# Grouped-query attention of a hybrid trunk: scores by queries for the maxima, scores by keys for the values

## The chip, the cores and the metric

The kernel runs on one core of one Trainium2 chip. The metric is device microseconds of one execution of the whole program, the median over several runs. The core has five engines that work beside each other, each through its own instructions in order: TensorE (PE, matrix products into PSUM), VectorE (DVE), ScalarE (ACT), GpSimd (POOL, which here also issues the row gathers), and SyncE (SP, which issues most of the DMAs). Everything is float32.

## The reference, cut to what matters

A trunk of two layers works on two groups of tokens: a prompt of 128 tokens and a sample of 512 tokens, both of width 1024. In each layer four mixers (grouped-query attention, RWKV-7, neighbourhood attention, gated DeltaNet) of 256 columns each stand beside each other, their outputs go through `w_out`, and then a sparse expert layer (PEER) follows. The mixer of this case is the first one, for the sample: 4 query heads of 64 columns share 2 key/value heads, and each of the 512 queries attends in one softmax to the 512 latent keys and to 128 cached context keys.

```python
def blocked_attention(q, k, v):
    def one_block(qblk):
        s = jnp.einsum("bkgqd,bkld->bkgql", qblk, k).astype(jnp.float32) * scale
        p = jax.nn.softmax(s, axis=-1).astype(v.dtype)
        return jnp.einsum("bkgql,bkld->bkgqd", p, v)
    ...
def gqa_mixer(p, lp, ctx_kv):
    ...
    q = rms_norm(q, lp["gqa_q_norm"]); k = rms_norm(k, lp["gqa_k_norm"])   # then rotary
    o = blocked_attention(qh, jnp.concatenate([kh, k_ctx], axis=2),
                              jnp.concatenate([vh, v_ctx], axis=2))
```

## The kernel before

The program is written with tiles: pools hand out buffers, and a scheduler orders the instructions of each engine by priorities and by a simulated run. Every engine then works through its list in order. A tile that takes over a buffer waits until the last reader of the earlier tile is done.

The stages of the sample are, for each layer: `s_mix` (input projections, then the four mixers), then `s_peer` (`w_out`, norm, expert layer). In `s_mix` the RWKV steps (names `s_R`, `s_U`, `s_dS`, `s_S`, `s_O`), the DeltaNet inverse (`s_Yt` and `s_BK` on DVE and POOL, then `s_Z`, `s_TZ`, `s_W`, `s_u` on PE), the DeltaNet steps and the neighbourhood attention `na` (`s_ns`) are independent chains that the scheduler interleaves with the attention `gqa`. The prompt's expert layer runs beside them: `p_back` gathers 128 rows of `u` and 128 rows of `v` per layer, one row per token and step (`p_gr`, issued by POOL, into a ring of three buffers), and DVE adds each (`ph<-p_gr,pac,ph`, 128x1024). After its last row, `p_back` takes two more buffers of that ring for `p_x` and `p_g`, loaded by SP, adds the residual on DVE, and in layer 0 stores it (`pxs<-p_x`).

Before the change, `gqa` (L575 to L682) does the following for the sample. After norm and rotary, queries and keys are transposed to `qT` and `kT` (64 rows of one head group in each half of the partitions). Then a loop of 16 turns, over 4 query tiles `t` and 4 heads `h`, goes in two halves; `skewed` emits the scores of a turn ahead of the values of the turn before.

- `scores`: one product of 64 rows with 512 columns (latent keys) and one with 128 columns (context keys) into a pair of PSUM banks `s_sc`; DVE takes the row maximum over 640 columns (`s_gmx`, L656); ACT takes the exponential of 128x640 with the row sum (`s_pr`).
- `values`: `soft_T` transposes the five 128x128 blocks of `s_pr` on PE back into the banks of `s_sc` (L328), ACT copies them (`s_pT`, 128x512, and `s_pTb`, 128x128), and five products with 64 columns of values sum into `s_po`.
- After the fourth head of a tile: reciprocal of the sums (128x4), one multiplication (`s_oat`), two transposes, two copies into `mixA`.

`mix_out` stores each mixer's output to memory (`smix`). In `s_peer`, `w_out` (L1469 to L1495) loads it back (`s_mix<-smix`) and loads the weights (`s_wo<-in_w_out_dram`), both by SP; its first product `s_wo<-s_wo,s_mix` begins the rest of the layer.

## Time and profile before

| what | value |
|---|---|
| median of the runs | 4911.13 us (4857.45 to 4959.15, 3 runs) |
| span of the profiled execution | 4964.6 us |
| PE busy | 4286.4 us (86%) |
| DVE busy | 3412.8 us (69%) |
| ACT busy | 1456.1 us (29%) |
| POOL busy | 1877.7 us (38%) |
| mean granted clock of TensorE | 0.844 |

The profiled execution is about 1.1% above the median and about 0.1% above the slowest of the three runs. In the rows further down, PE's matrix products appear as records: a product of float32 operands has two records, a transpose one. `s_sc<-s_kT,s_qT` names the tile that is written and the tiles that are read. [...] The attention of layer 0 lies at about 797 to 982 us, that of layer 1 at about 3197 to 3375 us.

### The profile page before, as it was taken

How to read it: one execution, taken by the hardware profiler on the slowest of the kernel's cores; microseconds unless marked ns; L12 is line 12 of the kernel's file. 1: busy time of each engine (PE TensorE's matmuls, PEld its weight loads, DVE VectorE, ACT ScalarE, POOL GpSimd, SP SyncE). 2: the span in 40 equal slices, each digit the busy share in tenths (PEclk: the TensorE clock that was granted, in tenths of full speed). 3: DMA queues.
4: the chain of work that ended last, by engine and by line, in shares of the span. 5: the costliest groups of instructions: out<-in, count | busy, mean ns of one | idle time of the engine just before them, and what ended most of it. 6: DMA issues, size and time to landing. Idle time of an engine off the chain costs nothing. (4 is left out here: it accounts for less than half of the span.)

```text
span 4964.6 us, 64764 instructions
## 1 busy us (share of the span) xinstructions
PE 4286.4 (86%) x21406; PEld 2957.0 (60%) x21406; DVE 3412.8 (69%) x8434; ACT 1456.1 (29%) x4149; POOL 1877.7 (38%) x1696
## 2 busy tenths in 40 slices
PE   7888878877698989999993688898769999999989
PEld 4454556665466854666672355666547788577563
DVE  2337875655899875664568677655489998894884
ACT  3322333331111840211110331433211174351340
POOL 0004443232443335443435443423144344463543
PEclk8888975556899989999996778555689999999979
DMA  7767885577797989997998879636679889999877
GB/s 263 261 203 244 272 259 162 156 204 271 265 342 263 359 292 366 362 363 269 364 357 277 274 262 284 194 114 192 239 256 325 299 306 327 340 357 342 328 261 284
DMA packets 500348, 1384.67 MB, mean 279 GB/s; under 512 B 109552, under 2 KB 167856, under 8 KB 498992
## 3 DMA queue, kind: packets, MB, share of 16 engines
q0 software_dynamic: 221184, 805.40, 47.5%
q1 hardware_dynamic: 215472, 531.29, 30.3%
q10 hardware_dynamic: 63360, 43.85, 2.8%
q8 instruction: 172, 2.82, 0.2%
q14 instruction: 160, 1.31, 0.1%
HBM read 1323.41 MB, written 56.93 MB: 278 GB/s over the span
## 5 line engine op out<-in xcount | busy, mean ns | idle before, releaser
L321 PE MATMUL s_us<-s_hT,s_uT 128*128 128x256 f32 x4096 | 964.2, 389 | 47.5 <-ACT s_pa L310 31.3
L1765 POOL DMA_INDIRECT s_gr<-in_peer_v_dram,s_ig x512 | 631.6, 1234 | 736.6 <-DVE s_acc L307 354.0
L1765 POOL DMA_INDIRECT s_gr<-in_peer_u_dram,s_ig x512 | 596.1, 1164 | 827.3 <-DVE s_gr L307 375.1
L321 PEld LDWEIGHTS s_us<-s_hT,s_uT 128*128 128x128 f32 x4096 | 775.5, 194 | 179.0 <-ACT s_pa L310 37.6
L307 DVE SCALAR_TENSOR_TENSOR s_acc<-s_gr,s_gact,s_acc 128x1024 f32<-128x1024 f32 x508 | 650.2, 1280 | 210.2 <-DMA s_gr<-in_peer_v_dram,s_ig 204.6
L307 DVE SCALAR_TENSOR_TENSOR s_gr<-s_gr,s_h 128x1024 f32<-128x1024 f32 x512 | 617.4, 1216 | 170.8 <-DMA s_gr<-in_peer_u_dram,s_ig 170.2
L321 PE MATMUL s_out<-s_v,s_pa 128*128 128x512 f32 x1408 | 625.7, 603 | 3.5 <-ACT s_gstg L310 2.2
L321 PE MATMUL s_cm<-s_hT,s_w 128*128 128x512 f32 (+3 forms) x1664 | 537.0, 478 | 24.8 <-ACT s_stg L310 17.4
L1765 POOL DMA_INDIRECT p_gr<-in_peer_v_dram,pig x256 | 262.2, 1024 | 615.2 <-DVE ph L307 340.7
L321 PEld LDWEIGHTS s_out<-s_v,s_pa 128*128 128x128 f32 x1408 | 268.5, 193 | 326.2 <-issue 322.0
L1765 POOL DMA_INDIRECT p_gr<-in_peer_u_dram,pig x256 | 290.4, 1134 | 443.4 <-DVE p_gr L307 247.0
L321 PEld LDWEIGHTS s_cm<-s_hT,s_w 128*128 128x128 f32 (+1 forms) x1664 | 281.7, 197 | 244.1 <-issue 148.8
L307 DVE SCALAR_TENSOR_TENSOR p_gr<-p_gr,ph 128x1024 f32<-128x1024 f32 x256 | 311.8, 1220 | 156.7 <-DMA p_gr<-in_peer_u_dram,pig 156.1
L307 DVE SCALAR_TENSOR_TENSOR ph<-p_gr,pac,ph 128x1024 f32<-128x1024 f32 x254 | 325.2, 1280 | 123.3 <-DMA p_gr<-in_peer_v_dram,pig 121.2
L310 ACT ACTIVATE s_hot<-consts,s_gT 128x128 f32<-128x128 f32 x768 | 271.8, 391 | 310.2 <-PE s_G L321 308.5
L321 PEld LDWEIGHTS s_G<-s_hot 128*128 128x128 f32 x2048 | 296.1, 210 | 93.8 <-ACT s_hot L310 28.2
L321 PE MATMUL s_G<-s_hot 128*128 128x42 f32 (+2 forms) x2048 | 305.8, 298 | 49.1 <-DVE s_hot L304 25.7
L304 DVE TENSOR_SCALAR s_hot<-consts,s_gT 128x42 f32<-128x42 f32 (+2 forms) x1024 | 281.5, 327 | 14.7 <-PE s_G L321 14.1
L321 PE MATMUL s_out<-s_v,s_p 128*128 128x512 f32 x640 | 287.3, 594 | 1.8 <-DMA s_v<-in_peer_v_dram 1.8
L310 ACT ACTIVATE s_hot<-s_hot,ones 128x128 f32<-128x128 f32 x768 | 267.4, 388 | 1.3
L321 PEld LDWEIGHTS s_out<-s_v,s_p 128*128 128x128 f32 x640 | 119.2, 190 | 127.1 <-issue 119.4
L328 PE MATMUL s_xT<-consts,s_xn 128*128 128x128 f32 x128 | 29.5, 378 | 184.1 <-ACT s_acc L293 84.6
(705 smaller groups left out, 6051.8 us busy)
## 6 DMA issues: line engine op xcount, KB each, us to landing
s_uT<-in_peer_uT_dram SPq DMA_DIRECT2D x256, 512.0 KB
s_v<-in_peer_v_dram SPq DMA_DIRECT2D x256, 512.0 KB
s_wm<-in_w_mod_dram SPq DMA_DIRECT2D x96, 512.0 KB
s_w<-in_peer_wq_dram SPq DMA_DIRECT2D x54, 512.0 KB
p_w<-in_w_in_dram SPq DMA_DIRECT2D x50, 512.0 KB
s_w<-in_w_in_dram SPq DMA_DIRECT2D x50, 512.0 KB
p_w<-in_peer_wq_dram SPq DMA_DIRECT2D x32, 512.0 KB
sproj<-s_stg ACTq DMA_DIRECT2D x50, 256.0 KB
```

Of the source, the lines that this page charges most:

```text
L304: self.nc.vector.tensor_scalar(out=out, in0=a, scalar1=s1, scalar2=s2, op0=op0, op1=op1)
L307: return self.nc.vector.scalar_tensor_tensor(out=out, in0=a, scalar=s, in1=b, op0=op0, op1=op1, **kw)
L310: self.nc.scalar.activation(out, in_, f, **kw)
L321: i = self.nc.tensor.matmul(out, lhsT, rhs, start=start, stop=stop)
L328: i = self.nc.tensor.transpose(out, in_, self.ident[b : b + n, b : b + n])
L1765: nc.gpsimd.indirect_dma_start(out=u, out_offset=None, in_=self.ap[f"{table}{l}"], in_offset=o)
```

## The change

The sample's attention moves into a new function, `gqa_ctx`. The prompt keeps the old path.

- Each key tile `ka` (and `kac` for the context keys) holds one key head in its 64 partitions, zeros in the other 64, and ones in one row of those. The query tile `Q` is kept four times (key head, query head), 128 rows each.
- `maxima(h)`: for each of the four query tiles the same score products as before (64 rows, 512 and 128 columns), the same DVE maximum (negated), then a product of the maxima's column with the identity, which gives a row of 128; ACT copies the row (1x128) into the row of `Q` that meets the row of ones.
- `values(h)`: for each of the five key blocks one product of 128 rows, keys as the stationary operand, with all 512 queries (`s_sT`). The row of ones brings the negated maximum in. ACT takes the exponential, 128x512, and one product of a 128x128 block of `vb` (64 columns of ones beside 64 columns of values) with 512 columns sums into `s_po`. Half of its rows are the sums, the other half the outputs. DVE takes a reciprocal of 64x512 and multiplies 64x512 into `mixA`, which needs no transpose.
- The 88 transposes per layer, the exponentials of 128x640 with their sums, the copies `s_pT` and `s_pTb`, and the 80 products with 64 columns are gone. New are, per layer, 16 products with one stationary column, 16 copies of 1x128, 40 products of 128x128 with 512 columns, 20 exponentials of 128x512, 4 reciprocals and 4 multiplications of 64x512, and 10 memsets on POOL. The values are loaded in pieces of 64 columns.

```diff
@@ -586,10 +586,20 @@
                 self.stt(tab[i][:, 1, :, 0:32], sin, -1.0, g2, ALU.mult, ALU.mult)
                 self.tt(tab[i][:, 1, :, 32:64], sin, g1, ALU.mult)
         qr = [a.rearrange("p (t k d) -> p t k d", k=2, d=64) for a in st.a1("qr")]
-        kr, vt = st.a1("kr")
-        self.pload(st, vt, 3)
+        if st.ctx:
+
+            kr = st.u1("kr")
+            vb = [st.wp.tile([P, 11, 64], F32, tag="w", name=st.nm("vb")) for _ in range(2)]
+            for kv, v in enumerate(vb):
+                cs = slice(64 * kv, 64 * kv + 64)
+                nc.gpsimd.memset(v[:, 0:11:2], 1.0)
+                nc.sync.dma_start(v[:, 1:9:2], st.proj[3].rearrange("p (t c) -> p t c", c=P)[:, :, cs])
+                nc.sync.dma_start(v[:, 9], self.ap["cgv"][l, :, cs])
+        else:
+            kr, vt = st.a1("kr")
+            self.pload(st, vt, 3)
+            vt = vt.rearrange("p (t c) -> p t c", c=P)
         kr = kr.rearrange("p (t h d) -> p t h d", h=2, d=64)
-        vt = vt.rearrange("p (t c) -> p t c", c=P)
         for ch in range(3):
             sq, qn = st.a1("qsq")
             self.pload(st, qn, ch)
@@ -618,6 +628,9 @@
         if not st.ctx:
             nc.scalar.dma_start(self.out["gk"][l].rearrange("k n d -> n k d"), kr[:, 0])
             nc.scalar.dma_start(self.out["gv"][l].rearrange("k n d -> n k d"), vt[:, 0].rearrange("p (k d) -> p k d", k=2))
+        if st.ctx:
+            self.gqa_ctx(st, l, qr, kr, vb)
+            return
         qT = st.a1("qT")
         kT, kc = st.a1("kT")
         for j in range(3):
@@ -630,55 +643,75 @@
             else:
                 self.act(qT[j], ps[:, :T], AF.Copy, scale=0.125)
         mixT = st.a1("mixA")
-        if not st.ctx:
-            heads = []
-            for h in range(4):
-                kv, j = h // 2, h % 2
-                rows = slice(64 * kv, 64 * kv + 64)
-                heads.append((qT[j][rows], kT[rows], vt[:, 0, 64 * kv : 64 * kv + 64]))
-            self.full_attn(st, heads, ([0, 1], [2, 3]), mixT)
-            self.mix_out(st, 0, mixT)
-            return
-        kc, vc = kc[:, :P], kc[:, P : 2 * P]
-        nc.sync.dma_start(kc, self.ap["cgk"][l])
-        nc.sync.dma_start(vc, self.ap["cgv"][l])
-        acc = {}
-
-        def scores(i):
-            t, h = i // 4, i % 4
+        heads = []
+        for h in range(4):
             kv, j = h // 2, h % 2
             rows = slice(64 * kv, 64 * kv + 64)
-            q = qT[j][rows, t * P : (t + 1) * P]
-            ps = st.pair("sc")
-            self.mm(ps[:, :T], q, kT[rows])
-            self.mm(ps[:, T : T + P], q, kc[rows])
-            m = st.asmall("gmx", 1)
-            nc.vector.tensor_reduce(out=m, in_=ps[:, : T + P], axis=AX.X, op=ALU.max, negate=True)
-            pr = st.asmall("pr", T + P)
-            if h == 0:
-                acc[t] = st.asmall("gsm", 4)
-            self.act(pr, ps[:, : T + P], AF.Exp, bias=m, accum_out=acc[t][:, h : h + 1])
-            return pr, ps
-
-        def values(i, prs):
-            pr, ps = prs
-            t, h = i // 4, i % 4
-            kv = h // 2
-            pT = self.soft_T(st, [pr[:, :T], pr[:, T:]], [ps[:, :T], ps[:, T:]])
-            if h == 0:
-                acc["po"] = st.out_psum("po")
-            po, sm = acc["po"], acc[t]
-            for kk in range(5):
-                v = vt[:, kk, 64 * kv : 64 * kv + 64] if kk < 4 else vc[:, 64 * kv : 64 * kv + 64]
-                self.mm(po[:, h * 64 : (h + 1) * 64], pT[kk], v, kk == 0, kk == 4)
-            if h == 3:
-                nc.vector.reciprocal(sm, sm)
-                o = st.u1("oat")[:, :256]
-                self.tt(o.rearrange("p (h d) -> p h d", h=4), po[:, :256].rearrange("p (h d) -> p h d", h=4),
-                        sm.unsqueeze(2).to_broadcast([P, 4, 64]), ALU.mult)
-                self.to_mix(st, mixT, o, t, po[:, 256:])
-
-        skewed(4 * NT, scores, values)
+            heads.append((qT[j][rows], kT[rows], vt[:, 0, 64 * kv : 64 * kv + 64]))
+        self.full_attn(st, heads, ([0, 1], [2, 3]), mixT)
+        self.mix_out(st, 0, mixT)
+
+    def gqa_ctx(self, st, l, qr, kr, vb):
+
+
+        nc, NT, T = self.nc, st.NT, st.T
+        half = lambda i: slice(64 * i, 64 * i + 64)
+        Q = [[st.u1("qT") for _ in range(2)] for _ in range(2)]
+        ka = [st.u1("ka") for _ in range(2)]
+        kac = st.u1("kac")[:, : 2 * P].rearrange("p (k n) -> p k n", k=2)
+        for kv in range(2):
+            for x in (ka[kv], kac[:, kv]):
+                nc.gpsimd.memset(x[half(1 - kv)], 0.0)
+                nc.gpsimd.memset(x[64 - 64 * kv : 65 - 64 * kv], 1.0)
+            nc.sync.dma_start(kac[half(kv), kv], self.ap["cgk"][l, half(kv)])
+        for j in (2, 0, 1):
+            ps = st.apsum("qkT")
+            for t in range(NT):
+                src = (kr if j == 2 else qr[j])[:, t]
+                self.tr(ps[:, t * P : (t + 1) * P], src.rearrange("p k d -> p (k d)"))
+            for kv in range(2):
+                if j == 2:
+                    self.evac(ka[kv][half(kv)], ps[half(kv), :T], "a")
+                else:
+                    self.act(Q[kv][j], ps[:, :T], AF.Copy, scale=0.125)
+        mixT = [st.u1("mixA") for _ in range(2)]
+
+        def maxima(h):
+            kv, j = h // 2, h % 2
+            m = st.asmall("gmx", NT)
+            r = slice(64 - 64 * kv, 65 - 64 * kv)
+            for t in range(NT):
+                ts = slice(t * P, (t + 1) * P)
+                ps = st.pair("sc")
+                q = Q[kv][j][half(kv), ts]
+                self.mm(ps[:, :T], q, ka[kv][half(kv)])
+                self.mm(ps[:, T : T + P], q, kac[half(kv), kv])
+                nc.vector.tensor_reduce(out=m[:, t : t + 1], in_=ps[:, : T + P], axis=AX.X, op=ALU.max, negate=True)
+                self.mm(ps[r, T + P : T + 2 * P], m[:, t : t + 1], self.ident)
+                self.evac(Q[kv][j][r, ts], ps[r, T + P : T + 2 * P], "a")
+
+        def values(h, _):
+            kv, j = h // 2, h % 2
+            po = st.out_psum("po")
+
+            def keys(kk):
+                ps = st.apsum("sT")
+                self.mm(ps, ka[kv][:, kk * P : (kk + 1) * P] if kk < NT else kac[:, kv], Q[kv][j])
+                pT = st.asmall("pr", T + P)[:, :T]
+                self.act(pT, ps, AF.Exp)
+                return pT
+
+            def value(kk, pT):
+                v = vb[kv][:, 2 * kk + 1 - j : 2 * kk + 3 - j].rearrange("p b d -> p (b d)")
+                self.mm(po, v, pT, kk == 0, kk == NT)
+
+            skewed(NT + 1, keys, value)
+            rc = st.u1("rc")
+            o = half(j)
+            nc.vector.reciprocal(rc[o], po[half(1 - j)])
+            self.tt(mixT[kv][o], po[o], rc[o], ALU.mult)
+
+        skewed(4, maxima, values)
         self.mix_out(st, 0, mixT)
```

The scheduler orders all engines anew. Three places of its order follow.

PE, layer 0, the stretch just after the RWKV steps. In the order of before, the last turns of the attention stand here (rows of transposes, `s_po` with 64 columns, scores):

```order
L321 MATMUL s_po_7039<-s_kT_6901,s_pTb_7079 128x64
L321 MATMUL s_sc_7087<-s_kT_6900,s_qT_6898 128x512
L321 MATMUL s_sc_7087<-s_kT_6901,s_qT_6898 128x128
L328 MATMUL s_sc_7066<-consts,s_pr_7071 128x128 x4
L321 MATMUL s_R_5743<-s_S_5719,s_AR_3445 64x128
...
L328 MATMUL s_sc_7066<-consts,s_pr_7071 128x128
L321 MATMUL s_po_7039<-s_kr_6852,s_pT_7095 128x64 x4
```

The changed kernel has there (`s_Z` is the first product of the DeltaNet inverse):

```order
L321 MATMUL s_Z_5983<-s_A_4760 32x32
L321 MATMUL s_sT_7104<-s_qT_6906,s_ka_6909 128x512
L321 MATMUL s_po_7095<-s_pr_7101,s_vb_6853 128x512
L321 MATMUL s_sT_7113<-s_qT_6906,s_kac_6910 128x512
L321 MATMUL s_sT_7104<-s_qT_6906,s_ka_6909 128x512
L321 MATMUL s_po_7095<-s_pr_7106,s_vb_6853 128x512
L321 MATMUL s_Z_5983<-s_A_4760 32x32 x31
L321 MATMUL s_po_7095<-s_pr_7110,s_vb_6853 128x512
```

Of the 40 wide products (`s_sT`, `s_po`) of layer 0, 15 stand among the RWKV steps (four such steps lie between the first of them and the last), and 25 behind the last RWKV step, with four of the 16 score pairs beside them. In layer 1, 22 wide products and three score pairs stand behind the last RWKV step, and about four RWKV steps and seven score pairs lie between the first wide product and the last RWKV step. In layer 0, most of the neighbourhood attention has moved behind the attention's end, among the DeltaNet steps.

SP, layer 0, the end of `s_mix` and the loads of `w_out`. Before:

```order
L355 DMA g2w_13116<-in_rw_g_dram 64x256
L1475 DMA s_mix_8480<-smix 128x1024
...
L1485 DMA s_wo_8492<-in_w_out_dram 128x1024
...
L1934 DMA sx_84<-s_x_8524 128x1024
L1860 DMA p_x_8430<-px_79 128x1024
```

After:

```order
L355 DMA g2w_12970<-in_rw_g_dram 64x256
...
L1893 DMA p_x_8284<-px_79 128x1024
L412 DMA p_g_795_8286<-grow 128x1024
L1831 DMA pxs<-p_x_8284 128x1024
L1508 DMA s_mix_8334<-smix 128x1024
...
L1518 DMA s_wo_8346<-in_w_out_dram 128x1024
```

The prompt's three DMAs, which wait for the last gathered rows, stood behind the loads of `w_out` and now stand ahead of them. On DVE, 24 additions of gathered rows stood behind the last DeltaNet step of layer 0, the last three of them behind the first norm after `w_out`; now 12 stand there, all ahead of `w_out`.

SP, layer 1, the same place. Before:

```order
L1860 DMA p_x_23251<-px_79 128x1024
L412 DMA p_g_1592_23253<-grow 128x1024
L1802 DMA p_fg_23257<-in_final_g_dram 128x1024
L1475 DMA s_mix_23310<-smix 128x1024
...
L1485 DMA s_wo_23322<-in_w_out_dram 128x1024
```

After:

```order
L1508 DMA s_mix_23018<-smix 128x1024
...
L1518 DMA s_wo_23042<-in_w_out_dram 128x1024
L1893 DMA p_x_22959<-px_79 128x1024
L1518 DMA s_wo_23046<-in_w_out_dram 128x1024
...
L412 DMA p_g_1592_22961<-grow 128x1024
```

Here the prompt's DMAs stood ahead of all loads of `w_out`; now `p_x` stands behind the first four weight tiles and ahead of the other four.

## Rows read from the trace of the kernel before

**Rows 1.** The page, 40 slices of the span, granted clock in tenths

```profile
PEclk8888975556899989999996778555689999999979
```

**Rows 2.** Busy time by stretch: stretch, length, each engine's busy (instructions), PEclk, DMA, GB/s

```profile
796.60:985.00 188.40, 175.39 (x666) 124.68 (x666) 104.07 (x222) 57.64 (x180) 45.38 (x45) 0.50 0.43 130
985.00:1075.00 90.00, 62.06 (x694) 54.72 (x693) 54.90 (x76) 34.03 (x99) 35.61 (x35) 0.57 0.79 228
3200.00:3275.00 75.00, 75.00 (x306) 53.78 (x304) 33.71 (x95) 21.77 (x54) 9.64 (x11) 0.50 0.25 76
3425.00:3475.00 50.00, 50.00 (x225) 37.60 (x225) 27.17 (x47) 13.47 (x39) 10.26 (x11) 0.50 0.43 125
4700.00:4760.00 60.00, 58.74 (x221) 33.00 (x220) 49.92 (x91) 25.31 (x84) 34.83 (x26) 1.00 0.93 335
```

**Rows 3.** Waits of PE, 796.6 to 985: total us, times, longest

```profile
PE s_sc L328 <- ACT s_pr L310: 10.4, 2, 8.4
```

**Rows 4.** Timeline of PE in the attention: start, us, operation, records [idle before]

```profile
864.09 1.11 PE L328 MATMUL s_sc<-consts,s_pr 128*128 128x128 f32 x4
...
865.72 0.63 PE L321 MATMUL s_dS<-s_tok,s_tok 64*128 64x128 f32 x2
...
869.79 2.50 PE L321 MATMUL s_sc<-s_kT,s_qT 64*128 64x512 f32 x4
872.22 0.69 PE L321 MATMUL s_O<-s_S,s_AR 128*64 128x128 f32 x2
...
874.69 0.47 PE L328 MATMUL s_sc<-consts,s_pr 128*128 128x128 f32 x1
874.96 1.81 PE L321 MATMUL s_po<-s_kr,s_pT 128*128 128x64 f32 x8
...
878.48 0.69 PE L321 MATMUL s_po<-s_kT,s_pTb 128*128 128x64 f32 x2
```

**Rows 5.** Timeline of PE in the expert layer, 4700 to 4760

```profile
4702.16 8.83 PE L321 MATMUL s_out<-s_v,s_pa 128*128 128x512 f32 x20
4710.83 1.88 PE L321 MATMUL s_G<-s_hot 128*128 128x42 f32 x16
```

**Rows 6.** Groups on DVE, 796.6 to 985: count | busy, mean ns | idle before

```profile
L675 DVE RECIPROCAL s_gsm<-s_gsm 128x4 f32<-128x4 f32 x4 | 0.7, 173 | 1.9 <-ACT s_pr L310 1.9
...
L307 DVE SCALAR_TENSOR_TENSOR ph<-p_gr,pac,ph 128x1024 f32<-128x1024 f32 x43 | 54.9, 1277 | 6.2 <-DMA p_gr<-in_peer_v_dram,pig 5.9
```

**Rows 7.** Line 1213 (a reciprocal), durations min/median/max in ns

```profile
L1213 DVE RECIPROCAL s_dnp<-s_dnp x2: 342/344/347, 505.3 to 2895.9; 128x32 f32<-128x32 f32 x2
```

**Rows 8.** Timeline of SP, end of the mixers in layer 0

```profile
1186.40 3.23 SPq L1485 DMA_DIRECT2D s_wo<-in_w_out_dram  x4
...
1220.28 0.33 SPq L1860 DMA_DIRECT2D p_x<-px  x1
...
1233.02 0.33 SPq L1798 DMA_DIRECT2D pxs<-p_x  x1
```

**Rows 9.** Timeline of PE, same stretch

```profile
1157.61 0.69 PE L321 MATMUL s_O<-s_U,s_QK 64*64 64x64 f32 x4
...
1191.31 7.58 PE L321 MATMUL s_wo<-s_wo,s_mix 128*128 128x512 f32 x12 [12.65 <-issue]
```

**Rows 10.** Timeline of DVE, same stretch

```profile
1218.98 3.91 DVE L307 SCALAR_TENSOR_TENSOR ph<-p_gr,pac,ph 128x1024 f32<-128x1024 f32 x3
```

**Rows 11.** Timeline of SP, end of the mixers in layer 1

```profile
3546.12 0.33 SPq L1860 DMA_DIRECT2D p_x<-px  x1
...
3552.25 2.10 SPq L1475 DMA_DIRECT2D s_mix<-smix  x4
```

**Rows 12.** Timeline of PE, same stretch

```profile
3564.13 15.89 PE L321 MATMUL s_wo<-s_wo,s_mix 128*128 128x512 f32 x32 [19.61 <-DMA s_wo<-in_w_out_dram]
```

**Rows 13.** Waits of SP, 3450 to 3570

```profile
SPq L1860 <- DMA p_gr<-in_peer_v_dram,pig: 15.3, 1, 15.3
```

## The prediction

> **What bounds the kernel now.** I read the page's slices first: each slice is 124 us, and the granted clock falls to 0.5 and 0.6 in slices 7 to 10 and 26 to 29 [rows 1]. These are the two `s_mix` stages, where the attention lies; elsewhere it is mostly 0.7 to 0.9. Then the busy time by stretch [rows 2]: in the attention of layer 0 PE is busy for 175.4 of 188.4 us at a clock of 0.50, in that of layer 1 for 75.0 of 75.0 us at 0.50. DVE has 104 and ACT 58 of the 188 us. Then PE's waits: two waits for the exponential, 10.4 us together, are nearly all of its idle time there [rows 3]. So PE's own products, at the lower clock, bound the attention, and the RWKV steps that share PE are paid in the same coin. Behind it, from 985 to 1075 us, PE is busy for only 62 of 90 us: there the DeltaNet inverse decides, a chain through DVE, POOL and memory that this change leaves alone. Two things follow. Taking work off ACT is worth nothing; taking columns off PE counts one for one. And the clock is worth as much as the columns: 75.0 of 75.0 us busy gave 0.50, while in the expert layer 58.7 of 60.0 us busy gave 1.00 [rows 2].
>
> **What PE loses and gains.** One turn of before (one query tile, one head) is read from the timeline [rows 4]. The score pair starts at 869.79 and the next row at 872.22: 2.43 us where the row says 2.50, so each row overlaps the next by 0.07. Four transposes 1.11, one more 0.47, eight records of value products 1.81, two more 0.69. Sum 6.58, less five overlaps of 0.07: 6.23 us. Sixteen turns make 99.7 us, the 8 output transposes at 0.27 (1.11/4) 2.2: **102 us per layer**, of which 39 us are scores.
>
> After it, at the same clock: the 16 score pairs stay, 39 us. The wide product, 128 rows by 128 columns with 512 columns, has rows only at the higher clock: 20 records from 4702.16 to 4710.83, so 0.87 us per product of two records [rows 5]. At half the clock I take twice that, 1.73 us; 40 of them make 69 us. The product with one stationary column has no row. It streams 128 columns, as a transpose (0.27) and one 64x128 product (0.63 less 0.07) do [rows 4]. I take 0.5, since it has two records, as the latter: 8 us, with 4 and 9 as bounds. Sum 116 us: **14 us more per layer**, if the clock stays at 0.50. The transposes that go were cheap, and the wide products run over all 512 queries with half of their array on zeros or on ones.
>
> **What the clock gives back.** The stretches with the full clock are those where products of 128 rows by 128 columns with many columns stand one behind another [rows 2, 5]; those at 0.50 are mixes of products with 64 rows or 64 columns and transposes [rows 2, 4]. After the change 25 wide products and 4 score pairs of layer 0 stand behind the last RWKV step, close together; in layer 1 it is 22 and 3. I read these by the former rows: 25 x 0.87 + 4 x 1.2 + 1 = 28 us saved in layer 0, 22 x 0.87 + 3 x 1.2 + 1 = 24 us in layer 1. The other 15 and 18 stand one or two at a time among RWKV steps, and I read those by the latter rows: nothing.
>
> [...]
>
> **What lies beside PE.** ACT loses the wide exponentials with their sums and the copies and gains 20 exponentials: it has 58 us in 188, so nothing on the path. DVE gets 4 reciprocals of 64x512. The rows are 173 ns for 4 columns and 344 for 32 [rows 6, 7], 6.1 ns per column, so by estimate 3.3 us each, and with the multiplication (at most the 1.28 of a 128x1024 addition [rows 6]) about 4.5. `s_po` has one buffer, so the next head's first value product waits for it; two to four wide products of the next head stand ahead of that, 2 to 7 us. I take nothing; with that cover gone it is 4 x 4.5 = 18 us per layer. The maxima now go from DVE straight back to PE; other products stand in between nearly everywhere. The memsets (POOL has 45 us in 188) and the smaller DMAs of the values come early: nothing.
>
> **What the new order moves.** In layer 0 SP now has `p_x`, `p_g` and `pxs` ahead of the loads of `w_out`. They wait for the last gathered rows. Before, DeltaNet's last step ended at about 1158.2 and `w_out` began at 1191.3, 33 us later [rows 9]; the gathering went on to 1222.9 [rows 10], `p_x` went out at 1220.28 and `pxs` at 1233.02 [rows 8]. The 24 additions behind the last step took 65 us, 2.7 each. Now 12 stand there: 32 us. The residual's two operations at up to 1.28 and `pxs` add 3, and the way from `s_mix` to the first product takes 11.9 us, as in layer 1 (3552.25 to 3564.13) [rows 11, 12]. So `w_out` starts 47 us after the step where it was 33: **14 us lost**. Bounds: at 1.28 per addition it is 15 + 15 = 30, so 3 us gained; at the 4.4 of the attention's stretch (43 additions in 188 us [rows 6]) 53 + 15 = 68, so 35 lost. In layer 1 the reverse: `p_x` waited 15.3 us for a gathered row [rows 13] and went out at 3546.12, `s_mix` only at 3552.25 [rows 11]. Now `s_mix` is not held: **5 us gained**, between 0 and 6.
>
> **Sum.** Layer 0: 14 - 28 + 14 = 0. Layer 1: 14 - 24 - 5 = -15. The profiled execution of 4964.6 us would become about 4950. The median of the runs shown is 4911.1, 1.1% below that execution; the same step makes it **4896 us**.
>
> **Rivals.**
> 1. *The clock stays at 0.50 throughout.* For it: full busy time at 0.50 [rows 2]; the wide products share PE with the DeltaNet inverse's small ones in just that place. Then layer 0 is +28 and layer 1 +9: 4948, slower than before.
> 2. *The gathering holds `w_out` of layer 0.* Place: `p_x` and `pxs` on SP. If the last addition still comes at 1222.9, `w_out` begins 15 us later, at 1238 where it was 1191: 47 us lost instead of 14, 4929, slower than before. It decides as soon as the last addition comes later than 15 us ahead of the time at which `w_out` could otherwise begin. For it: DVE works in order and the additions stand among products that wait for PE. Against: half as many stand at the end.
> 3. *The full clock from the first value product on.* Then 15 more wide products save 13 us in layer 0, four score pairs 5, and four RWKV steps half of 10.5 each ((175.4 - 102)/7 [rows 2, 4]), 21: layer 0 is -39. In layer 1, 18 products save 16, seven pairs 8, four steps 21: -60. Together 4812. Against: in this place the RWKV steps are half of the work.
> [...]
>
> **How the numbers follow.** Chances: the forecast 0.40, rival 1 0.20, rival 2 0.13, rival 3 0.17, rival 4 0.10. The prediction is 4896; its own range, with the one-column products (4 us lower, 1 higher per layer), the tail of layer 0 (17 lower, 21 higher) and layer 1's 5, is 4870 to 4925. The whole range reaches down past most of rival 3, to 4810, and up past rival 1 with the longest tail and part of the uncovered reciprocals (4948 + 21 + 15), to 4984. Faster by over 2% (under 4813, about what a measurement of this kernel can tell from no change) are rival 4 and part of rival 3: 0.15. Slower by over 2% (over 5009) needs rival 1, the long tail and all reciprocals on the path: 0.05. Within 2%: 0.80.
>
> **What would show it.** The granted clock behind the last RWKV step near 1.00, and before it 0.50; a wide product at 1.73 us among the RWKV steps and 0.87 behind them; the reciprocal near 3.3 us, with no wait of `s_po` for DVE; 12 additions and then `p_x`, `pxs`, `s_mix` in one chain ahead of `w_out` in layer 0. The prediction is wrong if the wide products stay at 1.73 everywhere, if the RWKV steps run at the full clock, if PE waits for the maxima or for the reciprocals, or if stages far from the attention, whose order the scheduler also shuffled, move by more than this change.

## The result and the profile after

The changed kernel takes 4904.9 us (median of 20 runs, 4862.92 to 4929.68), the kernel before 4878.08 in the same 20 rounds (4813.17 to 4959.15). The ratio is 1.008, 95% interval 1.0055 to 1.0106: within 2%, and measurably slower. The forecast was 0.3% faster. For the ratio, executions more than 1.5% above the fastest of their kernel are left out, seven of the 20 of before, so it stands above that of the plain medians, which differ by 27 us (0.55%).

The time falls inside the range of the prediction, but by luck: the prediction started from an execution that turned out not to be the usual one, and the median of before, from which its time was scaled, came out 33 us lower than the one it used. Its 4964.6 us are more than any of those 20 runs of before. Two more profiles of the unchanged kernel, b1 and b2, show other attention stages. Stage lengths from the traces, in us, from the first score product of a layer to the first product of `w_out`:

| kernel | layer 0 | layer 1 | span |
|---|---|---|---|
| before, the profile the prediction read | 394.6 | 368.3 | 4964.6 |
| before, again (b1; b2) | 339.4; 341.0 | 347.1; 317.8 | 4889.9; 4861.0 |
| after, and again (a1) | 349.7; 346.9 | 356.4; 361.5 | 4898.9; 4901.1 |
| x1_actq | 348.8 | 330.5 | 4874.4 |
| x2_recip | 323.1 | 323.9 | 4880.5 |
| x3_half | 353.7 | 321.3 | 4879.6 |
| x6_rows; z_after | 360.1; 337.8 | 290.5; 310.0 | 4867.9; 4855.6 |
| g0_first (new form in layer 0 only) | 365.2 | 373.7 | 4941.7 |
| g1_second (new form in layer 1 only) | 345.8 | 318.0 | 4856.0 |
| y0_pool; y2_rows | 384.4; 348.0 | 371.0; 314.2 | 4949.8; 4863.6 |
| y1_rows; z_before | 390.7; 387.2 | 376.7; 372.6 | 4964.7; 4926.5 |
| z2_before | 330.3 | 272.1 | 4816.5 |

Against the means of b1 and b2, the means of after and a1 are 8 us longer in layer 0 and 26 us longer in layer 1; the spans differ by 24.5, so about 10 us come back elsewhere. These means are of two executions each, and in layer 1 b1 and b2 are 29 us apart themselves; in layer 0 a third execution in before's order, that of g1_second, took 345.8.

Now the clock. The view is busy time by stretch (stretch, length, busy of PE, its weight loads, DVE, ACT and POOL with instructions, granted clock as a share of full speed, a mean over the stretch, DMA share, GB/s). The kernel before, in b1:

```profile
800.00:820.00 20.00, 20.00 (x77) 13.44 (x76) 11.77 (x28) 6.20 (x17) 6.67 (x6) 0.50 0.34 105
820.00:840.00 20.00, 19.90 (x138) 14.65 (x137) 15.10 (x33) 6.78 (x18) 7.00 (x8) 1.00 0.62 182
840.00:860.00 20.00, 19.98 (x140) 14.28 (x140) 16.44 (x33) 7.65 (x23) 5.71 (x7) 1.00 0.58 168
...
1040.00:1060.00 20.00, 20.00 (x98) 15.09 (x94) 12.60 (x24) 5.68 (x18) 3.75 (x4) 0.50 0.45 134
```

From 820 us on the attention of layer 0 has a clock of 1.00, with the same instructions in the same order that had 0.50 for 188 us in [rows 2]. PE was as good as fully busy in both up to 880 us (19.90 us or more of each 20). What this is worth shows in the DeltaNet inverse, whose part on DVE (61 pairs of operations) starts and ends so in layer 0, in the profile that the prediction read and in b1:

```profile
L298 DVE TENSOR_TENSOR s_Yt<-s_BK,s_BK x61: 164/252/296, 797.2 to 994.1; 128x110 f32<-128x110 f32 x5, 128x126 f32<-128x126 f32 x5, 128x120 f32<-128x120 f32 x5, 128x30 f32<-128x30 f32 x4
L298 DVE TENSOR_TENSOR s_Yt<-s_BK,s_BK x61: 165/254/293, 801.3 to 941.9; 128x110 f32<-128x110 f32 x5, 128x126 f32<-128x126 f32 x5, 128x120 f32<-128x120 f32 x5, 128x30 f32<-128x30 f32 x4
```

It ends 197 us behind the first score in the one and 141 in the other: the whole difference of some 55 us between the two is there by then. The changed kernel:

```profile
800.00:820.00 20.00, 14.03 (x62) 8.81 (x63) 13.42 (x31) 3.35 (x9) 6.90 (x8) 0.57 0.78 246
...
840.00:860.00 20.00, 20.00 (x83) 12.08 (x82) 18.09 (x39) 4.39 (x13) 7.17 (x9) 0.50 0.70 212
860.00:880.00 20.00, 20.00 (x100) 10.62 (x100) 15.36 (x32) 5.49 (x14) 6.94 (x8) 0.81 0.61 185
...
900.00:920.00 20.00, 20.00 (x92) 9.54 (x91) 18.04 (x36) 7.97 (x21) 8.70 (x7) 0.96 0.79 256
940.00:960.00 20.00, 12.72 (x158) 6.67 (x160) 13.01 (x11) 10.28 (x30) 9.62 (x9) 0.76 0.99 248
...
1040.00:1060.00 20.00, 20.00 (x97) 14.31 (x95) 10.02 (x18) 4.65 (x14) 3.79 (x4) 0.50 0.41 126
...
3160.00:3180.00 20.00, 20.00 (x70) 11.39 (x69) 11.29 (x25) 2.79 (x9) 3.78 (x4) 0.50 0.27 80
3200.00:3220.00 20.00, 19.98 (x110) 10.88 (x109) 17.81 (x34) 5.95 (x17) 3.78 (x4) 1.00 0.36 110
```

Its clock rises only where the wide products begin, 65 us after the first score in layer 0 and 49 in layer 1 (first score 799.9 and 3134.5), and in layer 0 it then goes back and forth (0.81, 0.96 and 0.76 in the stretches above). The DeltaNet steps with the neighbourhood attention (1040 to 1060) run at 0.50 with PE full in both kernels. Single instructions of after, on PE (start, us, records):

```profile
865.02 2.08 PE L321 MATMUL s_sT<-s_qT,s_ka 128*128 128x512 f32 x2
867.02 0.58 PE L321 MATMUL s_sc<-consts,s_gmx 128*1 128x128 f32 x2
...
946.38 1.02 PE L321 MATMUL s_sT<-s_qT,s_kac 128*128 128x512 f32 x2
947.24 1.02 PE L321 MATMUL s_sT<-s_qT,s_ka 128*128 128x512 f32 x2
...
961.56 3.78 PE L321 MATMUL s_sT<-s_qT,s_ka 128*128 128x512 f32 x4
965.13 2.62 PE L321 MATMUL s_po<-s_pr,s_vb 128*128 128x512 f32 x4
```

Start to start, the wide product takes 0.86 us where the clock is 1.00 (946.38 to 947.24), and 1.79 where it is 0.50 (two from 961.56 to 965.13; 2.00 where a one-column product follows). The reciprocals and who waits for them:

```profile
L711 DVE RECIPROCAL s_rc<-s_po x8: 3350/3352/3359, 887.0 to 3296.8; 64x512 f32<-64x512 f32 x8
L298 DVE TENSOR_TENSOR s_mixA<-s_po,s_rc x8: 672/689/694, 894.4 to 3301.5; 64x512 f32<-64x512 f32 x8
...
  PE s_po L321: 3.0, 1
```

And the end of the mixers of layer 0, SP's queue and then PE (the last neighbourhood output is transposed at 1133.46):

```profile
1123.26 0.33 SPq L1893 DMA_DIRECT2D p_x<-px  x1
...
1133.10 0.32 SPq L1831 DMA_DIRECT2D pxs<-p_x  x1
1133.47 8.99 SPq L1508 DMA_DIRECT2D s_mix<-smix  x4
```

```profile
1133.46 0.69 PE L328 MATMUL s_po<-consts,s_oat 128*128 128x128 f32 x2 [3.22 <-DVE s_oat L298]
1149.61 16.32 PE L321 MATMUL s_wo<-s_wo,s_mix 128*128 128x512 f32 x32 [15.46 <-DMA s_wo<-in_w_out_dram]
```

### The profile page after: what moved, and what is told of

Its sections match the earlier page's. It is cut to its first block, busy times and chain, and to the rows that moved or that the text cites. A ratio compares the mean times of both kernels' runs of the same rounds, so it can differ in the third digit from the quotient of the medians.

```text
span 4898.9 us, 64168 instructions
## 1 busy us (share of the span) xinstructions
PE 4223.8 (86%) x21134; PEld 2851.8 (58%) x21134; DVE 3439.7 (70%) x8434; ACT 1437.7 (29%) x4081; POOL 1912.3 (39%) x1716
## 5 line engine op out<-in xcount | busy, mean ns | idle before, releaser
L1798 POOL DMA_INDIRECT s_gr<-in_peer_v_dram,s_ig x512 | 647.1, 1264 | 696.9 <-DVE s_acc L307 327.0
```

Of the source, the lines that this page charges most:

```text
L1798: nc.gpsimd.indirect_dma_start(out=u, out_offset=None, in_=self.ap[f"{table}{l}"], in_offset=o)
```

## The experiments

**b1 and b2: the kernel before, profiled again.** No edit.

> The kernel before, unchanged, a second profile. Its 20 runs have a median of 4878 us, and the profiled execution of 4965 us was slower than all of them. Theory A (the prediction's reading holds): the attention of both layers again runs at a granted clock of 0.50 with PE busy all the time, first score to w_out takes 395 us in layer 0 and 367 us in layer 1, and the time that varies lies elsewhere. Theory B (the profiled execution was untypical just there): one or both mixer stages show a higher clock than 0.50 and take 40 us or more less, so that the time to be saved by the clock was not there in most runs.

> The kernel before, unchanged, a third profile, with the same expectations as the second: theory A says 395 and 367 us for the two mixer stages from first score to w_out at clock 0.50 in the attention; theory B says 40 us or more less in at least one of them, at a higher clock.

Measured: 4891.94 and 4862.93 us, layer 0 in 339.4 and 341.0, so theory B. Layer 1 took 347.1 and 317.8, in the same order: b2's clock came up 20 us earlier in its attention (0.78 in 3180 to 3200 us, b1's 0.50 there and 0.76 in the next 20) and was 1.00 for 40 us of its DeltaNet steps, where b1's was 0.50. Over 74 timed runs of before in the later sessions the mean granted clock goes from 0.840 (4978.9 us) to 0.876 (4833.5), and time and clock have a correlation of -0.97.

**a1: the changed kernel, profiled again.** No edit.

> The changed kernel, unchanged, a second profile. In the first one the stage from first score to w_out took 350 us in layer 0, with the clock between 0.65 and 1.00 from the first value product on. Theory A: the same again within 10 us in both layers, since the wide products always bring the clock up. Theory B: the stage varies by 20 us or more from one execution to the next, as it does in the kernel before.

Measured: 4902.86 us, both stages within 5 us of the first profile. Over its 20 runs after keeps a clock of 0.858 to 0.874. By a straight line through either kernel's runs, before takes 4872 us at 0.865 and after 4901: at the same mean clock about 29 us stay to be explained, by more than the clock.

**x1_actq: the prompt's last DMAs on another queue.** `p_x`, `p_g` and `pxs` are issued by ACT, so that `s_mix` no longer stands behind them on SP.

```diff
-            self.nc.sync.dma_start(x, st.x1)
+            self.nc.scalar.dma_start(x, st.x1)
```

> The changed kernel with the prompt's last loads and its store (p_x, p_g, pxs) issued by ACT instead of SP, so that SP's loads of w_out no longer stand behind the end of the gathering in layer 0. In two executions of the changed kernel w_out began 29 and 30 us after the neighbourhood attention's last scores. Theory S (that queue holds w_out): it begins 10 to 15 us earlier and the ratio to the kernel before falls from 1.008 to about 1.005. Theory N (the neighbourhood attention, now last, sets the end by itself): w_out moves by less than 5 us and the ratio stays at 1.007 to 1.009.

Measured: 4887.35 us, 1.0037 (1.0003 to 1.0071). PE's order in layer 0 stayed that of after, and there `w_out` came 348.8 us after the first score, no earlier. Behind the last transposes of the neighbourhood attention it came 12.0 us (1147.53 to 1159.48) instead of the 16.2 shown above: SP's queue costs 4 us, and the neighbourhood attention holds `w_out`. Layer 1 got 26 us shorter with the same attention and the same inverse: the scheduler had ordered it anew, and the clock there was 0.85 in the first 20 us after the first score, where after had 0.50.

**x2_recip: no division.** The reciprocal becomes a copy (the outputs are multiplied by the sums instead of divided).

```diff
-            nc.vector.reciprocal(rc[o], po[half(1 - j)])
+            nc.vector.tensor_copy(rc[o], po[half(1 - j)])
```

> The changed kernel with the four reciprocals of 64x512 per layer (3.35 us each on DVE) replaced by copies of the same shape, so the outputs are multiplied by the sums instead of divided. Theory D (VectorE's queue delays the DeltaNet inverse, whose end on DVE is 17 to 20 us later in layer 1 than before): that end comes about 10 us earlier in layer 1, ratio about 1.003 to 1.005. Theory P (PE's columns and their order set the time): less than 5 us, ratio 1.007 to 1.009.

Measured: 4888.02 us, 1.0030 (0.9993 to 1.0066). The order changed with it, and between 200 and 240 us after the first score of layer 0 the clock was 1.00 (0.78 and 0.50 in after), so the 27 us by which layer 0 got shorter cannot be given to the reciprocal. In layer 1 the inverse ended 7 us earlier on DVE, where theory D had 10. Inconclusive beyond this: after's own trace has one wait of 3.0 us behind the reciprocals.

**x3_half: half of the wide products' columns.** The products by keys, the exponentials and the value products take 256 of the 512 queries; the other half gets copies.

```diff
-                self.mm(ps, ka[kv][:, kk * P : (kk + 1) * P] if kk < NT else kac[:, kv], Q[kv][j])
+                self.mm(ps[:, : T // 2], ka[kv][:, kk * P : (kk + 1) * P] if kk < NT else kac[:, kv], Q[kv][j][:, : T // 2])
```

> The changed kernel with the wide products and exponentials over 256 of the 512 queries, while the reciprocals and multiplications stay as long as they were; half of the attention's outputs are thus copies. It takes 40 times about 0.43 us per layer at the full clock from PE. Theory P: 17 us per layer and more where the clock is low, ratio about 1.000. Theory D or N: at most half of it, ratio 1.004 or more.

Measured: 4872.45 us, 1.0020 (0.9983 to 1.0058). Forty products of a layer lost half of their columns, by estimate half of 0.86 to 1.79 us each and 17 to 36 us of PE; layer 0 took 353.7, as long as with them, while layer 1 came down to 321.3. The clock rose no earlier than in after (0.51 in 860 to 880 us, where after had 0.81). This does not price a column: the order was new in both layers, and from 100 to 160 us after the first score of layer 0 the clock was 0.50 to 0.59, where after had 0.73 to 0.95. It shows that the attention's products do not set the end of layer 0 by themselves: they were over 7 us earlier, and the inverse on DVE ended no earlier (the table under the next run).

**x6_rows: the scores for the maxima over 128 rows.** The same stage of after, with whole partitions (`Q` by `ka` with its zeros) instead of 64.

```diff
-                q = Q[kv][j][half(kv), ts]
-                self.mm(ps[:, :T], q, ka[kv][half(kv)])
-                self.mm(ps[:, T : T + P], q, kac[half(kv), kv])
+                q = Q[kv][j][:, ts]
+                self.mm(ps[:, :T], q, ka[kv])
+                self.mm(ps[:, T : T + P], q, kac[:, kv])
```

> The changed kernel with the score products for the maxima over all 128 rows, the other head's rows meeting zeros and one row of ones, which shifts each query's maximum by a constant that the softmax takes out again. The columns streamed are the same. Theory C (the clock comes up late, some 60 us behind the first score, because the maxima beside RWKV steps hold 64-row products, where the kernel before in its usual executions came up after some 20 us in layer 0): the full clock is there 30 to 40 us earlier, 15 to 20 us saved per layer, ratio 1.000 to 1.003. Else the clock comes up where it did and the ratio stays at 1.007 to 1.009.

Measured: 4865.52 us, 0.9963 (0.9921 to 1.0005), the median clock 0.8785 where after has 0.865. Its second stretch stands at the full clock:

```profile
820.00:840.00 20.00, 20.00 (x125) 12.73 (x124) 16.70 (x33) 4.72 (x15) 4.72 (x5) 1.00 0.48 137
```

The full clock came some 50 us earlier than in after, as theory C had it, but not the 15 to 20 us per layer. Layer 0 took 360.1 us, longer than in after; layer 1 took 290.5, 66 us less, with the inverse ending 28 us earlier and the DeltaNet steps at a mean clock of 0.97 where after had 0.50. The order was new in both layers. In layer 0, us from the first score:

| kernel | last value product of the attention | last operation of the inverse on DVE | first product of `w_out` |
|---|---|---|---|
| before, the profile the prediction read | 181 | 197 | 394.6 |
| before, again (b1) | 124 | 141 | 339.4 |
| after | 180 | 133 | 349.7 |
| x3_half | 173 | 135 | 353.7 |
| x6_rows | 125 | 150 | 360.1 |

In the two profiles in before's order the attention and the inverse are later together where the clock is 0.50 (181 and 197 us against 124 and 141). In the new orders the attention can end 56 us earlier (after to x6_rows) and `w_out` begins no earlier, because the inverse and the steps behind it do not come forward with it.

**z_after: x6_rows, and the neighbourhood attention's scores over 128 rows too.** Its queries are kept in two tiles, each with zeros in one half of the rows.

```diff
-            q = qT[c][rows, b * P : (b + 1) * P]
+            q = qz[h % 2][c][:, b * P : (b + 1) * P]
```

> The changed kernel with 128-row scores, and the scores of the neighbourhood attention over 128 rows too (queries kept twice, the other head zeroed). In most executions so far the stretch of DeltaNet steps and neighbourhood attention, about 100 us per layer, ran at 0.50 with PE busy all the time. Theory C: it now runs at 1.00 and each layer's mixers end 25 to 40 us earlier than in the changed kernel with 128-row scores, ratio to the kernel before 0.980 to 0.988. Theory W (the DeltaNet steps' own chain through DVE and PE sets that stretch): less than 10 us per layer, ratio 0.993 to 0.997.

Measured: 4851.87 us, 0.9933 (0.9906 to 0.9961), faster than before, but not by theory C's 1.2 to 2%. The stretch of DeltaNet steps had a mean clock of 0.77 and 0.82, not 1.00; layer 0 was 22 us shorter than in x6_rows, layer 1 20 us longer.

**y1_rows and z_before: the same on the old path.** Queries with zeros in the other half (four tiles instead of two), then the neighbourhood attention as well.

```diff
-            q = qT[j][rows, t * P : (t + 1) * P]
+            q = Qz[kv][j][:, t * P : (t + 1) * P]
-            self.mm(ps[:, :T], q, kT[rows])
+            self.mm(ps[:, :T], q, kT)
```

> The kernel before with one change: the queries are kept twice, each with the other head group's 64 rows zeroed, so that the score products run over all 128 rows; columns, transposes, exponentials and values stay as they were. Theory C (what decides the attention is whether the clock comes up beside the RWKV steps, which 128-row scores make sure of, the form of the attention hardly matters): the clock is 1.00 within 20 us of the first score in both layers, the slow executions of before vanish, the median falls by 20 to 40 us, ratio 0.992 to 0.996. Theory F (the new form itself brought the gain of the changed kernel with 128-row scores): ratio 0.998 to 1.002.

> The kernel before with 128-row scores in both attentions, the old path of the values kept. Against the changed kernel with the same two edits it tells what the new form is worth once the clock no longer differs. Theory C: both come out within 0.4% of each other, ratio to the kernel before 0.980 to 0.990. Theory P (the new form costs PE columns and moves the neighbourhood attention to the end): this one is the faster by 0.5% or more. Theory F: it is the slower by 0.5% or more.

Measured: 4951.92 us, 1.0141 (1.0083 to 1.0198), and 4930.19, 1.0109 (1.0054 to 1.0164). In y1_rows the last value products of the attention came 309 and 293 us after the first score, behind the DeltaNet steps: the two more query tiles took buffers that the second half of the attention waits for, and z_before is built alike. They say nothing on the rows.

**y2_rows and z2_before: the same with buffers for it.** The values and the context keys and values lie in the weight pool.

```diff
+            vt = st.wp.tile([P, 11, 64], F32, tag="w", name=st.nm("vt")).rearrange("p a b -> p (a b)")[:, :T]
+            kcv = st.wp.tile([P, 11, 64], F32, tag="w", name=st.nm("kcv")).rearrange("p a b -> p (a b)")
```

> The kernel before with 128-row scores in the attention, as in the run before the last, but with the values and the context moved to two buffers of the weight pool, so that the four query tiles have room and the attention stays among the RWKV steps. The old path of the values is kept. Theory C: the clock is 1.00 within 20 us of the first score in both layers, the slowest executions of before vanish, ratio 0.990 to 0.997. Theory F (the gain of the changed kernel with 128-row scores came from the new form): ratio 0.998 to 1.003.

> The same with 128-row scores in the neighbourhood attention as well, against the changed kernel with both edits, which came to 0.993. Theory C: 0.989 to 0.997, the form of the values is worth less than 0.4%. Theory P (the new form costs PE columns): 0.988 or less. Theory F: 0.998 or more.

Measured: 4839.53 us, 0.9943 (0.9905 to 0.9982), and 4818.58, 0.9883 (0.9782 to 0.9984). The last one beats both kernels, on the old path; its interval does not decide between theories C and P. In y2_rows the clock in layer 0 came up only 45 us after the first score, later than in b1 with 64 rows, and layer 0 took 348.0, as in after; what it gains by the profiles lies in layer 1 (314.2).

**y0_pool: these buffers with the old 64-row scores.**

> The kernel before with the values and the context keys and values in buffers of the weight pool, as in y2_rows, but its 64-row scores kept: what of y2_rows' 0.9943 is the other buffers and the other order they bring. Theory C (the 128-row scores bring it, by an earlier full clock): 0.998 to 1.002, the clock at 0.50 for some 50 us after the first score or throughout. Theory O (the other order brings it): 0.994 as y2_rows.

Measured: 4948.24 us, 1.0182 (1.0149 to 1.0216): 109 us more than y2_rows, and 76 more than before itself, by the medians of its session. The scheduler ordered y0_pool and y2_rows differently, so the two differ by more than the rows. One stretch of each, y0_pool first:

```profile
840.00:860.00 20.00, 20.00 (x85) 14.38 (x86) 15.05 (x32) 5.74 (x17) 6.67 (x7) 0.50 0.71 212
```

```profile
840.00:860.00 20.00, 20.00 (x139) 14.36 (x138) 15.91 (x33) 7.05 (x22) 5.46 (x6) 1.00 0.50 154
```

PE is full in both; at 1.00 it gets through 139 records where it was 85. The buffers alone bring no gain. That the rows of zeros bring the clock is the author's estimate from all the profiles together: in the twelve attention stages with 128-row scores (x6_rows, z_after, y1_rows, z_before, y2_rows, z2_before) the clock came up within 60 us of the first score, while of the ten on the old path with 64-row scores five stayed at 0.50 for the first 180 us after the first score (both of the profile that the prediction read, both of y0_pool, layer 1 of g0_first) and five came up earlier (both of b1, both of b2, layer 0 of g1_second). No pair of these runs differs in the rows alone.

**g0_first and g1_second: the new form in one layer.** The other layer keeps the old path.

```diff
+        new = st.ctx and l == 0
-        if st.ctx:
+        if new:
```

> The new attention in layer 0 only; layer 1 keeps the old path. PE's order up to the end of layer 0 is that of the changed kernel, layer 1 is ordered anew (neither before's nor after's). Theory N (the loss is the new form in layer 0: neighbourhood attention last, w_out 29 us behind it): first score to w_out 345 to 350 us in layer 0, where the two further profiles of before had 339 and 341, and a total 8 to 12 us above before, about 4890, ratio 1.002. Theory L (the loss sits in layer 1): as before in total, 1.000, with 318 to 347 us in layer 1. Theory O (any new order of a layer costs or gives 20 us, whatever the form): layer 1 outside 318 to 347.

> The new attention in layer 1 only; all engines' order up to the end of layer 0 is that of before, layer 1 is ordered anew (neither before's nor after's). Theory N (the loss sits in layer 0): layer 0 339 to 341 us as in the further profiles of before (or 395 where the clock stays at 0.50), the total as before, 1.000. Theory L (the new form costs in layer 1): 356 to 362 us in layer 1 and 1.003 or more. Theory O (the order of layer 1 decides, not the form): layer 1 below 345 us, total at or under that of before.

Measured: g0_first 4921.35 us, 1.0120 (1.0088 to 1.0151); g1_second 4869.88, 1.0017 (0.9979 to 1.0055). g1_second's layer 0 is in before's order and took 345.8, b1's time within 7 us and a1's within 2; its layer 1 has the new form in an order of its own and took 318.0, as short as the better of before's two. So the new form need not cost anything in layer 1: in another order than after's it took 38 us less. g0_first has after's order in layer 0 (365.2, with the clock lower than in after) and an old attention in layer 1 that stays at 0.50 through it (373.7): the old form too can be that slow in another order. That is what theory O expected of layer 1 in both runs.

What differs in after's layer 1 is the DeltaNet inverse. Its part on DVE starts and ends so (first and last start; the layer's first score at 3134.5 in after, 3135.6 in g1_second, 3136.0 in x1_actq, 3140.0 in b1, 3140.5 in b2). After, then g1_second, x1_actq, b1 and b2:

```profile
L298 DVE TENSOR_TENSOR s_Yt<-s_BK,s_BK x61: 175/252/294, 3161.8 to 3269.2; 128x110 f32<-128x110 f32 x5, 128x126 f32<-128x126 f32 x5, 128x120 f32<-128x120 f32 x5, 128x30 f32<-128x30 f32 x4
```

```profile
L298 DVE TENSOR_TENSOR s_Yt<-s_BK,s_BK x61: 175/252/293, 3147.0 to 3223.2; 128x110 f32<-128x110 f32 x5, 128x126 f32<-128x126 f32 x5, 128x120 f32<-128x120 f32 x5, 128x30 f32<-128x30 f32 x4
```

```profile
L298 DVE TENSOR_TENSOR s_Yt<-s_BK,s_BK x61: 168/255/300, 3152.1 to 3247.0; 128x110 f32<-128x110 f32 x5, 128x126 f32<-128x126 f32 x5, 128x120 f32<-128x120 f32 x5, 128x30 f32<-128x30 f32 x4
```

```profile
L298 DVE TENSOR_TENSOR s_Yt<-s_BK,s_BK x61: 174/256/294, 3148.9 to 3261.5; 128x110 f32<-128x110 f32 x5, 128x126 f32<-128x126 f32 x5, 128x120 f32<-128x120 f32 x5, 128x30 f32<-128x30 f32 x4
```

```profile
L298 DVE TENSOR_TENSOR s_Yt<-s_BK,s_BK x61: 161/255/295, 3149.0 to 3253.1; 128x110 f32<-128x110 f32 x5, 128x126 f32<-128x126 f32 x5, 128x120 f32<-128x120 f32 x5, 128x30 f32<-128x30 f32 x4
```

Counted from the first score it ends at 135, 88, 111, 122 and 113 us, and `w_out` follows 222, 230, 220, 226 and 205 us later. In the first four the length of layer 1 goes with the end of the inverse nearly one for one; in b2 the way behind it is some 20 us shorter, with the clock at 1.00 in part of its DeltaNet steps. With a1 (139, then 223) this splits the 26 us between the means of after and before: 20 have come about by the end of the inverse (137 against 117), 7 behind it. What DVE waits for in the first 140 us of the layer, in after and in g1_second (us, times, longest):

```profile
DVE s_gmx L689 <- PE s_sc L321: 16.4, 7, 5.7
DVE s_U L298 <- PE s_R L321: 9.7, 7, 3.2
```

```profile
DVE s_gmx L732 <- PE s_sc L321: 1.2, 1, 1.2
```

In after the inverse's operations stand in DVE's order among maxima that wait 16.4 us for scores; in g1_second the wait is 1.2 us. The clock of the first 60 us, 0.50, 0.50 and 0.73 by 20 us in after and 0.50, 0.50 and 0.65 in g1_second, does not explain this difference. That the order makes the 20 us is read from three orders of one form, not from an edit of the order alone; no run holds the order fixed and changes the form.

## Why the prediction was wrong

The forecast was 0.3% faster, and the kernel got slower: 0.8% by the ratio, 0.55% by the plain medians. That is the size of rival 1 (4948 against 4911, 0.75%), but not its mechanism, since the clock did not stay at 0.50 (0.96 in 900 to 920 us).

**The step that failed is "What bounds the kernel now".** It took the 0.50 of one execution [rows 2] for the kernel's own property. In three of four profiles of this order (b1, b2, and g1_second in layer 0) the old attention of layer 0 runs at 1.00 from 20 us after its first score, so most of its 102 us shrink there, by estimate to little more than half (from 840 to 860 us, with PE full, 78 records in that execution and 140 in b1), and the 28 us of "What the clock gives back" had mostly been given before the change; in layer 1 it comes to 1.00 later, within 80 us. The rivals' prices hang on the same base. That the execution stood above all three runs shown, while those runs were 102 us apart, could have been seen: that spread was more than six times the 15 us that the change was to save.

**"Taking columns off PE counts one for one"**, of the same step, was not borne out in the new orders: in x6_rows the attention of layer 0 ended 56 us earlier than in after and the layer did not shorten, and in x3_half half of the wide columns went and it did not shorten either. Whether it holds at 0.50 throughout no run tried.

**The scaling of the sum to the median** failed with it. Against the execution that it was worked out from, the sum was 0 and -15; the profile of after shows -45 and -12. Layer 1 agrees. Layer 0 is rival 3 (-39) rather than the forecast: the clock at the wide products among the RWKV steps had come up in part (0.81 in 860 to 880). Against the usual executions it is +8 and +26.

**"What PE loses and gains"**: right in kind. The one-column product takes about half a microsecond (estimate 0.5). The wide product is 1.79 us at 0.50 where 1.73 was taken, 0.86 at 1.00 where 0.87 was. By these the step's own sum says that the new form has more for PE, not less; how much in all was not measured.

**"What the clock gives back"**: as forecast, the clock is well above 0.50 behind the last RWKV step (912.5 us), at 0.76 in 940 to 960 rather than 1.00; the small products of the inverse and waits of PE lie there too.

**"What lies beside PE"**: right, but for the maxima. The reciprocal takes 3.35 us (3.3 estimated), the multiplication 0.69, and PE waits for them once, 3.0 us. For the maxima, taken at nothing, PE waits 4.4 us in layer 0 and 4.1 in layer 1.

**"What the new order moves", layer 0**: the size held, its cause only in part. `w_out` begins 49 us behind the last DeltaNet step (1100.5 to 1149.6), 47 were forecast. By x1_actq SP's queue is 4 us of it; the rest goes with the neighbourhood attention. It stood behind the attention's end in both orders; what changed is that its last scores now come 20 us behind the last DeltaNet step, where in b1 they came 37 us ahead of it. The price of an addition was misread, without harm: the trace of before has 18 additions, not 24, behind DVE's last DeltaNet operation, and the last three of them waited for the norm, not for rows. In after 12 stand there, and the last ends 26 us behind the last step, where 32 were taken. **Layer 1**: `w_out` begins 47 us behind the last DeltaNet step where it was 51 [rows 12], 4 us gained for 5. What the step missed there is the inverse on DVE: it looked at the loads of `w_out` and not at what the new order put ahead of that chain, which in after ended 13 to 22 us later than in b1 and b2.

**Rival 4**, 0.10 of the chances and most of the 0.15 for over 2% faster: no run shows a ground for this share. In the changed kernel PE ran no transpose at all between 820 and 860 us and the clock was 0.50; in b1 45 transposes of the old attention lie between 820 and 880 us and the clock was 1.00.

**What stays open.** Why the same program gets 0.50 in one execution and 1.00 in the next is not known from these runs. Of the 8 us of layer 0 the form's and the order's share were not told apart (the last DeltaNet step came 2 to 9 us earlier than in b1 and b2, the way from there to `w_out` was 11 to 17 us longer), and the further 10 us that come back outside the two stages were not followed.

## What to carry to other kernels

One profile is one execution: before a sum is built on its clock, compare its time with the spread of the runs, and if they differ by more than the change is worth, take a second profile. Where PE is full at 0.50 with products over 64 rows, filling the other rows with zeros is a cheap trial; here it gave 2.2% at the same buffers (y0_pool to y2_rows, in a new order) but 0.6% against before, whose attention in layer 0 reached 1.00 without it in three of four profiles, where the rewritten attention lost 0.8%. And when a scheduler orders all engines anew, look for the chain that decides the stage (here the inverse on DVE) in the new order, also where the change doesn't touch it.

## What the runs showed of the hardware

The granted clock of one stretch of one program differed between executions, 0.50 throughout in one and 1.00 from 20 us on in two others, worth 54 us in layer 0 (394.6 against 340.2). Products with 64 more rows of zeros, with as many columns and PE as busy (20.00 of 20 us), had 1.00 where those over 64 rows had 0.50 (y2_rows and y0_pool, 840 to 860 us); the order differed too. And 64-row scores do not rule 1.00 out: b1 has it in the same stretch.
